# Queries times states in three bfloat16 parts on 32 columns per sequence, and state updates on 32 rows per sequence, in one layer of an mLSTM and convolution decoder

## The chip, the cores and the metric

The kernel runs on one core of a Trainium2 chip. The metric is the device time of one execution in microseconds, the median of several runs. Where a time inside the execution is given, it is counted from the start of the profiled span.

## The reference

One layer projects 512 prompt tokens and 64 sample tokens (8 sequences of 8 new tokens) with one matrix, runs an mLSTM over 4 heads of 256 on one half of the columns and a gated causal convolution on the other half, and projects the result. The change touches the mLSTM of the sample tokens. Each of their 8 sequences brings a state per head, a 256 x 256 matrix C and a vector n. With q, k, v of the 8 new tokens the reference computes

```
s   = (q @ k.T) * exp(dmat - m_t)
num = w_inter * (q @ C) + s @ v
den = w_inter * (q @ n) + sum(s)
h   = num / max(|den|, exp(-m_t))
C_new = decay * C + sum_s ws[s] * outer(k[s], v[s])
n_new = decay * n + sum_s ws[s] * k[s]
```

followed by a layer norm over each head. The new states are outputs. All inputs and outputs are float32.

## The kernel before

TensorE works on float32 data with float32r matmuls: every operand is split into a high part and the rest, and a product is the sum of three matmuls (high x high, high x rest, rest x high). The split is an `activation` copy on ScalarE into the high part and a subtraction on VectorE for the rest.

The program is written as one list in the order of the main projection. `ORDER` names 61 column tiles; for each tile (a "unit of 16") the loop in lines 892 to 904 runs k from 0 to 15. One k is six matmuls (`proj`, line 184): three of 256 columns and three of 320. At every fourth k, ahead of the matmuls, `split` (lines 76 to 90) splits the weights that are due 12 k later: ScalarE L85, VectorE L86, with rings of `RING = 4` buffers; every second split also issues a weight load on SP (`load`). After k = 15, `evac` copies or gates the tile out of PSUM on ScalarE (L200, L202, L757) and VectorE (L763).

Everything else is hung into this list by `at(s, k, f)`: function f is issued behind the matmuls of tile s, index k (lines 656 to 700). No scheduler moves anything: each engine executes its instructions in the order in which they are issued, and waits where an operand or a buffer is not ready. In what follows, step n of a head is the n-th k counted from the one at which `b_SV(h, 0)` stands, `o` in line 687 (for heads 1 to 3 a weight split falls on steps 2, 6, 10 and so on and an `evac` between steps 5 and 6 and between 21 and 22; for head 0 splits fall on steps 0, 4, 8 and evacs ahead of steps 8 and 24).

For one head, the steps that matter here are: `b_SV` (prompt scores times values, L549) at steps 0 to 6, `head_ln` (layer norm of the prompt rows, line 572) at step 7, `b_KV` (L557) at 8 and 10, `b_hT` (transposes, L598) at 14 and 16. For the sample tokens `b_q` (line 455) writes the scaled queries into `QM`, high part in columns 0 to 7 and rest in columns 64 to 71 of a 128-column block per sequence. `c_split` (line 377) splits a state into `Chi` and `Clo`. `b_sC` (line 603), once per sequence b at steps 12, 16, ... 40, multiplies shifted windows of `QM` with both parts (L611, four matmuls of 258 columns, all 128 rows and columns), so that all sequences accumulate in one PSUM tile `ns`; the first call adds the in-chunk part (`Es` times `vs`, L614). Every second call also makes the state updates of two sequences (L623: four matmuls of 32 rows x 128 columns, 256 columns of right side), VectorE merges them with the decayed states (L629), POOL stores them (L630) and SP loads the next two states. `b_sLN` (line 634) copies `ns` out at step 42, moves its lower 64 rows to the upper ones with a DMA, and does the layer norm at step 48; `b_shT` follows at step 66. Small PSUM tiles `mi` rotate through three buffers.

Of the kernel before, what the change touches and what calls it, by code (L numbers as in the profile page):

```python
# [6 lines left out]

F32 = mybir.dt.float32
F32R = mybir.dt.float32r
AF = mybir.ActivationFunctionType  # L10
OP = mybir.AluOpType
PSUM = bass.MemoryType.PSUM

P = 128
# [3 lines left out]
NB, T8 = 8, 8  # L18
TS = NB * T8
# [3 lines left out]
NH = 4  # L23
DH = 256
# [31 lines left out]
def hybrid(ctx, tc, x0, wg0, wu, wgate, cpack, gpack, sct, hist, xres, lnp,  # L56
           o_y, o_ys, o_C, o_m, o_cs, o_ns, o_ms, o_cv, o_cvs):
    nc = tc.nc
    pe, act, dve, pool = nc.tensor, nc.scalar, nc.vector, nc.gpsimd
    main = ctx.enter_context(tc.tile_pool(name="main", bufs=1))  # L60
    dramp = ctx.enter_context(tc.tile_pool(name="dram", bufs=1, space=bass.MemoryType.DRAM))
# [91 lines left out]
    def mi(shape=(P, 512)):  # L153
        return psum.tile(list(shape), F32, name="mi", tag="mi", bufs=3)
# [7 lines left out]
    def ns_tile():  # L162
        return psum.tile([P, 512], F32, name="ns", tag="ns", bufs=1)
# [24 lines left out]
    KQV = {}  # L188
# [16 lines left out]
    g0t = new_phase("g0")  # L205
# [6 lines left out]
            nc.sync.dma_start(xr[k], x0[k])  # L212
            nc.sync.dma_start(wr[k], wg0[k])

    warm = g0t([P, 512], mybir.dt.bfloat16, "warm")
    dve.memset(warm, 1.0)
    wps = ns_tile()
    for _ in range(8):
# [47 lines left out]
    for k in range(KT):  # L266
        for n, x in enumerate((XH, XL)):
            for b in range(2):
                c0, c1 = SPANS[b]
# [97 lines left out]


    m = {}
    CS, CH = {}, {}  # L370

    def c_load(i):
        if i < NH * NB:
            CS[i] = m["t"]([P, 2, 258], F32, "Ct", bufs=5)
            nc.sync.dma_start(CS[i], sct[i])

    def c_split(i):
        if i < NH * NB:
            CH[i] = [m["t"]([P, 2, 258], F32R, n, bufs=2) for n in ("Chi", "Clo")]
            act.activation(CH[i][0], CS[i], AF.Copy)  # L380
            dve.tensor_sub(CH[i][1], CS[i], CH[i][0])  # L381

    def rb_load(h):
        m["RB"] = m["t"]([P, TOK + TS], F32, "RB")
# [5 lines left out]
    def open_m():  # L390
        t = m["t"] = new_phase("m2")
        m["vs"] = t([TS, 258], F32, "vs")
        m["QM"] = t([P, 2 * NB, P], F32R, "QM")
        pool.memset(m["vs"][:, 256:257], 1.0)
        pool.memset(m["vs"][:, 257:258], 0.0)
        pool.memset(m["QM"].bitcast(F32), 0.0)
        rb_load(0)
        for i in range(5):
            c_load(i)

    def b_E(h, part):
# [52 lines left out]

    def b_q(h):

        q, QM = KQV["q", h], m["QM"]
        qw = m["t"]([P, 2, TS], F32, "qw")
        for d in range(2):
            pool.tensor_tensor(out=qw[:, d], in0=q[:, d, S:], in1=m["RB"][:, TOK:], op=OP.mult)  # L460
        qv = qw.rearrange("p d (b t) -> p (d b) t", t=T8)
        act.activation(QM[:, :, 0:T8], qv, AF.Copy)
        dve.tensor_sub(QM[:, :, TS:TS + T8], qv, QM[:, :, 0:T8])

    def b_kT(h, a):
        if a == 0:
# [133 lines left out]
        hT[e] = mt([P, TOK], F32, f"hT{e}", tag="hT", bufs=8)  # L600
        act.activation(hT[e][:, :S], ps, AF.Copy, scale=hn_g[:, e:e + 1])

    def b_sC(h, b):
        if b == 0:
            m["ns"] = ns_tile()
        i = NB * h + b
        ch, cl = CH.pop(i)
        for d in range(2):
            w = m["QM"].rearrange("p a c -> p (a c)")[:, d * NB * P + b * 120:d * NB * P + b * 120 + P]
            for n, c in enumerate((ch, cl)):  # L610
                pe.matmul(m["ns"][:, :258], lhsT=w, rhs=c[:, d], start=b == 0 and d == 0 and n == 0,  # L611
                          stop=b == NB - 1 and d == 1 and n == 1)
            if b == 0 and d == 0:
                pe.matmul(m["ns"][:TS, :258], lhsT=m["Es"], rhs=m["vs"], start=False, stop=False)  # L614
        c_split(i + 1)
        if b % 2 == 0:
            return
        pss = []
        for bb in (b - 1, b):
            g, j = divmod(bb, 4)  # L620
            ps = mi((P, 2, DH))
            for d in range(2):
                pe.matmul(ps[:, d], lhsT=m["kS"][32 * j:32 * j + 32, g, d * P:(d + 1) * P],  # L623
                          rhs=m["vS"][32 * j:32 * j + 32, g], start=True, stop=True)
            pss.append(ps)
        for bb, ps in zip((b - 1, b), pss):
            ct = CS.pop(NB * h + bb)
            c = ct[:, :, :DH]
            dve.scalar_tensor_tensor(c, c, m["dec", h][:, bb:bb + 1], ps, op0=OP.mult, op1=OP.add)  # L629
            pool.dma_start(o_cs[NB * h + bb], c)  # L630
        c_load(i + 4)
        c_load(i + 5)

    def b_sLN(h, part):
        if part == 0:
            nsb, m["t2"] = m["t"]([P, 1, 258], F32, "nsb"), m["t"]([TS, 258], F32, "nsl")
            act.activation(nsb[:, 0], m["ns"][:, :258], AF.Copy)
            act.dma_start(m["t2"], nsb[TS:, 0])
            m["nsb"] = nsb
        else:  # L640
            nums = m["nums"] = m["nsb"][:TS]
            dve.tensor_add(nums[:, 0], nums[:, 0], m["t2"])
            head_ln(nums, TS, 1, CTs[:, 1, h:h + 1])

    def b_shT(h):
# [10 lines left out]
    def at(s, k, f, *a):  # L656
        s, k = s + k // KT, k % KT
        beside.setdefault((s, k), []).append((f, a))
# [5 lines left out]
    for h in range(NH):  # L664
# [27 lines left out]
        at(o[0], o[1] + 10, b_KV, h, 1)  # L692
        at(o[0], o[1] + 14, b_hT, h, 0)
        at(o[0], o[1] + 16, b_hT, h, 1)
        at(o[0], o[1] + 5, c_split, NB * h)
        for i in range(NB):
            at(o[0], o[1] + 12 + 4 * i, b_sC, h, i)
        at(o[0], o[1] + 42, b_sLN, h, 0)
        at(o[0], o[1] + 48, b_sLN, h, 1)
        at(o[0], o[1] + 66, b_shT, h)  # L700


# [402 lines left out]
```

## Time and profile before

| | before |
|---|---|
| median of 3 runs | 1145.35 us (1145.32 to 1145.37) |
| profiled execution | 1145.27 us |
| its span | 1143.3 us, 19722 instructions |
| TensorE busy | 1130.3 us, 99% of the span |
| VectorE busy | 722.0 us, 63% |
| ScalarE busy | 406.1 us, 36% |
| GpSimd busy | 147.0 us, 13% |

The span is the time from the first to the last instruction that the profiler recorded. Busy times count overlapping instructions once. Matmuls are pipelined, so the duration of one (some 0.3 us) is longer than the distance to the next.

### The profile page before, as it was taken

How to read it: one execution, taken by the hardware profiler on the slowest of the kernel's cores; microseconds unless marked ns; L12 is line 12 of the kernel's file. 1: busy time of each engine (PE TensorE's matmuls, PEld its weight loads, DVE VectorE, ACT ScalarE, POOL GpSimd, SP SyncE). 2: the span in 40 equal slices, each digit the busy share in tenths (PEclk: the TensorE clock that was granted, in tenths of full speed). 3: DMA queues.
4: the chain of work that ended last, by engine and by line, in shares of the span. 5: the costliest groups of instructions: out<-in, count | busy, mean ns of one | idle time of the engine just before them, and what ended most of it. 6: DMA issues, size and time to landing. Idle time of an engine off the chain costs nothing.

```text
span 1143.3 us, 19722 instructions
## 1 busy us (share of the span) xinstructions
PE 1130.3 (99%) x8062; PEld 1085.9 (95%) x8062; DVE 722.0 (63%) x1207; ACT 406.1 (36%) x772; POOL 147.0 (13%) x217
## 2 busy tenths in 40 slices
PE   9999999999999999999999999999999999999996
PEld 8999999999999999999999999999999988888895
DVE  6385455455355445428899998999977872433447
ACT  5335453345344443422222222222236651221224
POOL 0022030011002003101010111111203310000004
PEclk9999999999999999999999999999999999999998
DMA  8114262253245224222223222222222246632229
GB/s 292 68 57 132 77 195 86 77 185 96 74 134 168 67 74 160 86 87 90 93 92 108 87 100 85 85 81 75 93 93 75 92 145 188 205 143 93 70 87 166
DMA packets 43659, 127.50 MB, mean 112 GB/s; under 512 B 5372, under 2 KB 10108, under 8 KB 43120
## 3 DMA queue, kind: packets, MB, share of 16 engines
q1 hardware_dynamic: 37712, 112.44, 30.0%
q0 software_dynamic: 4992, 12.94, 4.3%
q8 instruction: 63, 1.03, 0.4%
q10 hardware_dynamic: 864, 0.85, 0.3%
q14 instruction: 28, 0.23, 0.1%
HBM read 110.11 MB, written 18.72 MB: 113 GB/s over the span
## 4 chain that ended last, share of the span: by engine, by line
PE 99%; DVE 1%; issue 0%; DVEq 0%
PE pp L184 71%; PE pp L977 3%; PE pp L978 3%; PE pp L979 3%; PE mi L978 2%; PE mi L979 2%; PE mi L977 2%; PE ns L611 1%; PE mi L442 1%; PE mi L974 1%; PE mi L973 1%; PE mi L549 1%; PE mi L184 1%; PE mi L557 1%; PE mi L623 1%; PE ns L979 0%
## 5 line engine op out<-in xcount | busy, mean ns | idle before, releaser
L184 PE MATMUL pp<-xh,whi 128*128 128x256 f32 (+1 forms) x1952 | 423.3, 298 | 0.0
L184 PE MATMUL pp<-xl,whi 128*128 128x256 f32 (+1 forms) x1952 | 416.5, 295 | 0.0
L184 PE MATMUL pp<-xh,wlo 128*128 128x256 f32 (+1 forms) x1952 | 415.5, 295 | 0.0
L86 DVE TENSOR_TENSOR wlo<-raw,whi 128x512 fp32r<-128x512 f32 x300 | 221.8, 742 | 266.9 <-ACT whi L85 266.5
L85 ACT ACTIVATE whi<-raw 128x512 fp32r<-128x512 f32 x300 | 188.5, 632 | 391.9 <-PE pp L184 246.1
L184 PEld LDWEIGHTS pp<-xh,wlo 128*128 128x128 f32 x1952 | 326.7, 188 | 0.0
L184 PEld LDWEIGHTS pp<-xl,whi 128*128 128x128 f32 x1952 | 326.4, 188 | 0.0
L184 PEld LDWEIGHTS pp<-xh,whi 128*128 128x128 f32 x1952 | 321.6, 189 | 3.0 <-issue 0.3
L724 DVE SCALAR_TENSOR_TENSOR Y<-U,cp,Y 128x512 f32<-128x512 f32 x240 | 189.8, 791 | 5.3
L978 PE MATMUL pp<-whi,mx 128*128 128x512 f32 (+1 forms) x128 | 46.9, 366 | 0.0
L977 PE MATMUL pp<-whi,mx 128*128 128x512 f32 (+1 forms) x128 | 46.9, 366 | 0.0
L979 PE MATMUL pp<-wlo,mx 128*128 128x512 f32 (+1 forms) x128 | 46.8, 366 | 0.0
L630 POOL DMA_DIRECT2D o_cs<-Ct x32 | 22.5, 717 | 181.9 <-DVE Ct L629 181.9
L381 DVE TENSOR_TENSOR Clo<-Ct,Chi 128x516 fp32r<-128x516 f32 x35 | 25.7, 733 | 27.4 <-ACT Chi L380 27.4
L757 ACT ACTIVATE sg<-pp,cp 128x256 f32<-128x256 f32 (+1 forms) x48 | 21.4, 496 | 45.4 <-PE pp L184 45.4
L978 PE MATMUL mi<-whi,mx 128*128 128x512 f32 (+1 forms) x96 | 36.1, 376 | 0.0
L977 PE MATMUL mi<-whi,mx 128*128 128x512 f32 (+1 forms) x96 | 36.0, 375 | 0.0
L979 PE MATMUL mi<-wlo,mx 128*128 128x512 f32 (+1 forms) x96 | 36.0, 375 | 0.0
L979 PEld LDWEIGHTS pp<-wlo,mx 128*128 128x128 f32 x128 | 24.1, 188 | 4.3
L977 PEld LDWEIGHTS pp<-whi,mx 128*128 128x128 f32 x128 | 24.1, 188 | 4.3
L978 PEld LDWEIGHTS pp<-whi,mx 128*128 128x128 f32 x128 | 24.0, 188 | 4.3
L1005 POOL DMA_DIRECT2D o_ys<-zs x4 | 3.4, 1184 | 188.9 <-ACT zs L1004 188.9
(334 smaller groups left out, 1370.1 us busy)
## 6 DMA issues: line engine op xcount, KB each, us to landing
raw<-wu SPq DMA_DIRECT2D x154, 512.0 KB, 3.3
Ct<-sct SPq DMA_DIRECT2D x32, 258.0 KB, 2.8
o_cs<-Ct POOLq DMA_DIRECT2D x32, 256.0 KB, 2.8
xr<-x SPq DMA_DIRECT2D x16, 288.0 KB, 5.0
z<-xres SPq DMA_DIRECT2D x8, 512.0 KB, 5.9
wr<-wg SPq DMA_DIRECT2D x16, 192.0 KB, 5.1
o_y<-z POOLq DMA_DIRECT2D x11, 256.0 KB, 7.6
o_y<-lnp SPq DMA_DIRECT2D x2, 1024.0 KB, 10.0
```

The costliest lines, as they stand in the source:

```text
L85: act.activation(hi, r, AF.Copy)
L86: (eng or dve).tensor_tensor(out=lo, in0=r, in1=hi, op=OP.subtract)
L184: pe.matmul(out[b], lhsT=w, rhs=x[:, slice(*SPANS[b])], start=k == 0 and n < 2, stop=k == KT - 1 and n >= 4)
L381: dve.tensor_sub(CH[i][1], CS[i], CH[i][0])
L442: pe.matmul(dst[J], lhsT=m[k_][:, d, J * P:(J + 1) * P], rhs=m[q_][:, d, J * P:S], start=d == 0 and n == 0, stop=d == 1 and n == 2)
L549: pe.matmul(ps[:, :258], lhsT=m[p_][:, o:o + P], rhs=m[v_][:, J], start=J == 0 and n == 0, stop=J == I and n == 2)
L630: pool.dma_start(o_cs[NB * h + bb], c)
L724: dve.scalar_tensor_tensor(y, u, w, y, op0=OP.mult, op1=OP.add)
L757: act.activation(sg[:, c0:c1], ps, AF.Sigmoid, bias=b_in[:, c:c + 1])
L977: pe.matmul(ps, lhsT=h_, rhs=hi, start=first, stop=False)
L978: pe.matmul(ps, lhsT=l_, rhs=hi, start=False, stop=False)
L979: pe.matmul(ps, lhsT=h_, rhs=lo, start=False, stop=last)
```

## The change

The queries are split into three bfloat16 parts (`Q`: 24 of 32 columns per sequence and d), and so is each state (`c0`, `c1`, `c2`, made by `c_split` with two ScalarE and two VectorE operations). `b_qC(h, r)` handles four sequences at once: each sequence's 32 query columns are the stationary operand on its own strip of 32 columns of TensorE's array, and its three parts stream by; rows 0 to 7, 8 to 15 and 16 to 23 of a strip collect the products of the three query parts. The result goes to SBUF, by DMA to `nsd` in DRAM, and comes back as three [64, 258] terms (`n3`), which are added to `nums`. `b_sKV(h, r)` makes the state updates of four sequences, in an order in which neighbouring matmuls lie on different 32-row strips and in different PSUM banks. `c_load` has eight buffers instead of five; `c_next` loads four states of the next head.

```diff
-    CS, CH = {}, {}
+    CS = {}
+    nsd = [dramp.tile([4, 4, T8, 2, 258], F32, name=f"nsd{h}") for h in range(NH)]
...
-            CS[i] = m["t"]([P, 2, 258], F32, "Ct", bufs=5)
+            CS[i] = m["t"]([P, 2, 258], F32, "Ct", bufs=8)
...
     def c_split(i):
-        if i < NH * NB:
-            CH[i] = [m["t"]([P, 2, 258], F32R, n, bufs=2) for n in ("Chi", "Clo")]
-            act.activation(CH[i][0], CS[i], AF.Copy)
-            dve.tensor_sub(CH[i][1], CS[i], CH[i][0])
+        j = i % 4
+        if j == 0:
+            for n, tag in (("c0", "Ph"), ("c1", "Pl"), ("c2", None)):
+                m[n] = m["t"]([P, 4, 2, 258], BF16, n, tag=tag)
+        c0, c1, c2 = (m[n][:, j] for n in ("c0", "c1", "c2"))
+        r = m["t"]([P, 2, 258], F32, "cr")
+        act.activation(c0, CS[i], AF.Copy)
+        dve.tensor_sub(r, CS[i], c0)
+        act.activation(c1, r, AF.Copy)
+        dve.tensor_sub(c2, r, c1)
...
     def b_q(h):
-        act.activation(QM[:, :, 0:T8], qv, AF.Copy)
-        dve.tensor_sub(QM[:, :, TS:TS + T8], qv, QM[:, :, 0:T8])
+        p_ = [Q.rearrange("p d b c -> p (d b) c")[:, :, i * T8:(i + 1) * T8] for i in range(3)]
+        act.activation(p_[0], qv, AF.Copy)
+        dve.tensor_sub(qv, qv, p_[0])
+        act.activation(p_[1], qv, AF.Copy)
+        dve.tensor_sub(p_[2], qv, p_[1])
...
-    def b_sC(h, b):
...
+    def b_qC(h, r):
+        if r == 0:
+            m["nsb"] = m["t"]([P, 2, 258], F32, "nsb")
+        ps = mi()
         for d in range(2):
+            for n in ("c0", "c1", "c2"):
+                for j in range(4):
+                    pe.matmul(ps[32 * j:32 * j + 32, :258], lhsT=m["Q"][:, d, 4 * r + j], rhs=m[n][:, j, d],
+                              start=d == 0 and n == "c0", stop=d == 1 and n == "c2")
+        act.activation(m["nsb"][:, r], ps[:, :258], AF.Copy)
+        if r:
+            act.dma_start(nsd[h].rearrange("j i t r e -> (j i t) r e"), m["nsb"])
+
+    def b_sKV(h, r):
+        pss = [mi((P, 2, DH)) for _ in range(3)] + [ns_tile().rearrange("p (d e) -> p d e", d=2)]
+        for d in range(2):
+            for j in range(4):
+                rows = slice(32 * j, 32 * j + 32)
+                pe.matmul(pss[j][:, d], lhsT=m["kS"][rows, r, d * P:(d + 1) * P], rhs=m["vS"][rows, r],
+                          start=True, stop=True)
+        for j in range(4):
+            b = 4 * r + j
+            c = CS.pop(NB * h + b)[:, :, :DH]
+            dve.scalar_tensor_tensor(c, c, m["dec", h][:, b:b + 1], pss[j], op0=OP.mult, op1=OP.add)
+            pool.dma_start(o_cs[NB * h + b], c)
+
+    def c_next(h, r):
+        for j in range(4):
+            c_load(NB * (h + 1) + 4 * r + j)
...
     def b_sLN(h, part):
         if part == 0:
-            nsb, m["t2"] = m["t"]([P, 1, 258], F32, "nsb"), m["t"]([TS, 258], F32, "nsl")
-            act.activation(nsb[:, 0], m["ns"][:, :258], AF.Copy)
-            act.dma_start(m["t2"], nsb[TS:, 0])
+            ps = mi()
+            pe.matmul(ps[:TS, :258], lhsT=m["Es"], rhs=m["vs"], start=True, stop=True)
+            m["nums"] = m["t"]([TS, 1, 258], F32, "nums")
+            act.activation(m["nums"][:, 0], ps[:TS, :258], AF.Copy)
+        elif part == 1:
+            m["n3"] = m["t"]([TS, 3, 258], F32, "n3", tag="cr")
+            for r in range(2):
+                for j in range(4):
+                    b = 4 * r + j
+                    nc.sync.dma_start(m["n3"][b * T8:(b + 1) * T8], nsd[h][j, :3, :, r].rearrange("i t e -> t i e"))
...
-        at(o[0], o[1] + 5, c_split, NB * h)
-        for i in range(NB):
-            at(o[0], o[1] + 12 + 4 * i, b_sC, h, i)
-        at(o[0], o[1] + 42, b_sLN, h, 0)
-        at(o[0], o[1] + 48, b_sLN, h, 1)
+        for r in range(2):
+            for j in range(4):
+                at(o[0], o[1] + (7, 19)[r] + (0, 1, 2, 4)[j], c_split, NB * h + 4 * r + j)
+            at(o[0], o[1] + (18, 31)[r], b_qC, h, r)
+            at(o[0], o[1] + (21, 35)[r], b_sKV, h, r)
+            at(o[0], o[1] + (27, 41)[r], c_next, h, r)
+        at(o[0], o[1] + 25, b_sLN, h, 0)
+        at(o[0], o[1] + 42, b_sLN, h, 1)
+        at(o[0], o[1] + 52, b_sLN, h, 2)
```

ScalarE's order in head 1 from the layer norm of the prompt rows (`sm`) on, before the change (`kv` and `hT` are evictions, `whi` a weight split, `q` a projection tile's eviction):

```order
L566 ACTIVATE sm_2699<-sm_2699 128x4
L560 ACTIVATE kv<-mi 128x258
L85 ACTIVATE whi<-raw 128x512
L560 ACTIVATE kv<-mi 128x258
L380 ACTIVATE Chi<-Ct 128x516
L85 ACTIVATE whi<-raw 128x512
L601 ACTIVATE hT_2826<-mi,cp 128x512
L601 ACTIVATE hT_2845<-mi,cp 128x512
L380 ACTIVATE Chi<-Ct 128x516
L85 ACTIVATE whi<-raw 128x512
```

The same place in the changed kernel (`c_2778` is `c0`, `c_2779` is `c1` of the first four states):

```order
L578 ACTIVATE sm_2750<-sm_2750 128x4
L387 ACTIVATE c_2778<-Ct 128x516
L389 ACTIVATE c_2779<-cr 128x516
L572 ACTIVATE kv<-mi 128x258
L387 ACTIVATE c_2778<-Ct 128x516
L389 ACTIVATE c_2779<-cr 128x516
L387 ACTIVATE c_2778<-Ct 128x516
L389 ACTIVATE c_2779<-cr 128x516
L86 ACTIVATE whi<-raw 128x512
L572 ACTIVATE kv<-mi 128x258
L387 ACTIVATE c_2778<-Ct 128x516
L389 ACTIVATE c_2779<-cr 128x516
```

Four splits of states, two operations each, now stand together behind the layer norm, ahead of the evictions and weight splits that stood there.

VectorE's order in head 1 from the last operation of the layer norm on, before the change (`wlo` is a weight split):

```order
L592 TENSOR_SCALAR num<-num,mv_2701,sm_2699 128x256 x4
L86 TENSOR_TENSOR wlo<-raw,whi 128x512
L381 TENSOR_TENSOR Clo<-Ct,Chi 128x516
L86 TENSOR_TENSOR wlo<-raw,whi 128x512
L381 TENSOR_TENSOR Clo<-Ct,Chi 128x516
L629 SCALAR_TENSOR_TENSOR Ct<-Ct,dec,mi 128x2x256 x2
```

The second four states in the changed kernel (`cr` is `r`, `c_2962` is `c2`):

```order
L87 TENSOR_TENSOR wlo<-raw,whi 128x512 x2
L388 TENSOR_TENSOR cr<-Ct,c_2960 128x516
L390 TENSOR_TENSOR c_2962<-cr,c_2961 128x516
L388 TENSOR_TENSOR cr<-Ct,c_2960 128x516
L390 TENSOR_TENSOR c_2962<-cr,c_2961 128x516
L640 SCALAR_TENSOR_TENSOR Ct<-Ct,dec,mi 128x2x256 x3
L640 SCALAR_TENSOR_TENSOR Ct<-Ct,dec,ns 128x2x256
L388 TENSOR_TENSOR cr<-Ct,c_2960 128x516
L390 TENSOR_TENSOR c_2962<-cr,c_2961 128x516
L87 TENSOR_TENSOR wlo<-raw,whi 128x512
L388 TENSOR_TENSOR cr<-Ct,c_2960 128x516
L390 TENSOR_TENSOR c_2962<-cr,c_2961 128x516
```

The state updates of the first four sequences stand in the middle of the splits of the second four.

## Rows read from the trace of the kernel before

**Rows 1.** Page: span, busy time of each engine, engines of the chain that ended last.
```profile
span 1143.3 us, 19722 instructions
...
PE 1130.3 (99%) x8062; PEld 1085.9 (95%) x8062; DVE 722.0 (63%) x1207; ACT 406.1 (36%) x772; POOL 147.0 (13%) x217
...
PE 99%; DVE 1%; issue 0%; DVEq 0%
```

**Rows 2.** TensorE's groups by shape: instructions x count, busy us, mean ns, idle before.
```profile
L611 PE MATMUL ns<-Chi,QM 128*128 128x258 f32 x64 | 17.6, 295 | 0.0
L611 PE MATMUL ns<-Clo,QM 128*128 128x258 f32 x64 | 16.9, 282 | 0.0
...
L623 PE MATMUL mi<-vS,kS 32*128 32x256 f32 x64 | 8.1, 328 | 0.0
```

**Rows 3.** Timeline of TensorE, head 1, steps 12 to 17: start us, length us, what.
```profile
224.69 0.28 PE L611 MATMUL ns<-Chi,QM 128*128 128x258 f32 x1
...
225.94 0.43 PE L184 MATMUL pp<-xh,whi 128*128 128x256 f32 x2
...
227.54 0.60 PE L598 MATMUL mi<-ident,num 128*128 128x128 f32 x4
227.89 0.51 PE L184 MATMUL pp<-xh,whi 128*128 128x256 f32 x2
...
230.24 0.28 PE L611 MATMUL ns<-Chi,QM 128*128 128x258 f32 x1
230.35 0.28 PE L611 MATMUL ns<-Clo,QM 128*128 128x258 f32 x1
230.56 0.50 PE L623 MATMUL mi<-vS,kS 32*128 32x256 f32 x4
231.00 0.53 PE L184 MATMUL pp<-xh,whi 128*128 128x256 f32 x2
231.37 0.42 PE L184 MATMUL pp<-xl,whi 128*128 128x256 f32 x2
```

**Rows 4.** Timeline of VectorE, head 1, last operation of the layer norm on.
```profile
221.29 1.38 DVE L592 TENSOR_SCALAR num<-num,mv,sm 128x256 f32<-128x256 f32 x4
222.59 0.69 DVE L86 TENSOR_TENSOR wlo<-raw,whi 128x512 fp32r<-128x512 f32 x1
224.28 0.69 DVE L381 TENSOR_TENSOR Clo<-Ct,Chi 128x516 fp32r<-128x516 f32 x1 [1.00 <-ACT Chi L380]
...
232.06 1.40 DVE L629 SCALAR_TENSOR_TENSOR Ct<-Ct,dec,mi 128x512 f32<-128x512 f32 x2
```

**Rows 5.** Timeline of ScalarE, head 1.
```profile
223.62 0.63 ACT L380 ACTIVATE Chi<-Ct 128x516 fp32r<-128x516 f32 x1
...
235.74 0.89 ACT L202 ACTIVATE q<-pp,cp 128x256 f32<-128x256 f32 x2 [2.75 <-PE pp L184]
```

**Rows 6.** Timelines, heads 0 and 3: end of the layer norm, step 13, table load.
```profile
133.14 1.39 DVE L592 TENSOR_SCALAR num<-num,mv,sm 128x256 f32<-128x256 f32 x4
...
136.92 0.28 PE L611 MATMUL ns<-Chi,QM 128*128 128x258 f32 x1
...
422.39 0.28 PE L611 MATMUL ns<-Chi,QM 128*128 128x258 f32 x1
...
422.51 1.38 DVE L592 TENSOR_SCALAR num<-num,mv,sm 128x256 f32<-128x256 f32 x4
...
430.71 1.28 ACT L757 ACT_TABLE_LOAD   x1
```

**Rows 7.** Page, DMA issues: KB each, median us from issue to landing.
```profile
raw<-wu SPq DMA_DIRECT2D x154, 512.0 KB, 3.3
```

**Rows 8.** Stretches: us, busy us of each engine (instructions), granted clock, DMA.
```profile
205.00:255.00 50.00, 50.00 (x383) 48.37 (x382) 24.81 (x55) 19.90 (x40) 4.20 (x6) 1.00 0.41 128
...
1134.00:1136.00 2.00, 0.00 (x0) 0.00 (x0) 1.93 (x7) 0.00 (x0) 0.00 (x0) 1.00 1.10 221
1136.00:1138.00 2.00, 0.00 (x0) 0.00 (x0) 2.00 (x3) 0.00 (x0) 0.00 (x0) 0.60 1.09 237
```

More of the change, by code (lines that the diff above doesn't have):

```diff
@@ L9 @@
 F32R = mybir.dt.float32r
+BF16 = mybir.dt.bfloat16
 AF = mybir.ActivationFunctionType
@@ L213, in g0_load @@
             nc.sync.dma_start(wr[k], wg0[k])
-    warm = g0t([P, 512], mybir.dt.bfloat16, "warm")
+    warm = g0t([P, 512], BF16, "warm")
     dve.memset(warm, 1.0)
@@ L392, in open_m @@
         m["vs"] = t([TS, 258], F32, "vs")
-        m["QM"] = t([P, 2 * NB, P], F32R, "QM")
+        m["Q"] = t([P, 2, NB, 32], BF16, "Q")
         pool.memset(m["vs"][:, 256:257], 1.0)
         pool.memset(m["vs"][:, 257:258], 0.0)
-        pool.memset(m["QM"].bitcast(F32), 0.0)
+        pool.memset(m["Q"], 0.0)
         rb_load(0)
-        for i in range(5):
+        for i in range(8):
             c_load(i)
@@ L455, in b_q @@
     def b_q(h):
-        q, QM = KQV["q", h], m["QM"]
+        q, Q = KQV["q", h], m["Q"]
         qw = m["t"]([P, 2, TS], F32, "qw")
@@ L601, in b_hT @@
         act.activation(hT[e][:, :S], ps, AF.Copy, scale=hn_g[:, e:e + 1])
-    def b_sC(h, b):
[L604 to L607, printed above, removed]
-        for d in range(2):
[L609 to L632, printed above, removed]
@@ L634, in b_sLN @@
+    def c_next(h, r):
+        for j in range(4):
+            c_load(NB * (h + 1) + 4 * r + j)
     def b_sLN(h, part):
         if part == 0:
-            nsb, m["t2"] = m["t"]([P, 1, 258], F32, "nsb"), m["t"]([TS, 258], F32, "nsl")
-            act.activation(nsb[:, 0], m["ns"][:, :258], AF.Copy)
-            act.dma_start(m["t2"], nsb[TS:, 0])
-            m["nsb"] = nsb
-        else:
-            nums = m["nums"] = m["nsb"][:TS]
-            dve.tensor_add(nums[:, 0], nums[:, 0], m["t2"])
+            ps = mi()
[8 more added lines that the diff above has]
+                    nc.sync.dma_start(m["n3"][b * T8:(b + 1) * T8], nsd[h][j, :3, :, r].rearrange("i t e -> t i e"))
+        else:
+            nums = m["nums"]
+            for i in range(3):
+                dve.tensor_add(nums[:, 0], nums[:, 0], m["n3"][:, i])
```

## The prediction

> **What bounds the kernel.** I read the page first: TensorE is busy for 99% of the span, and the chain that ended last is 99% PE [rows 1]. So the time changes only by what TensorE executes or waits for, and any new wait costs its full length. I then read TensorE's groups by shape. The work that the change replaces is 128 queries-times-states matmuls (L611) and 64 state updates (L623) [rows 2]. Their durations, 282 to 328 ns, overlap and are no price; the price is the distance between starts, from the timeline of head 1 [rows 3]. Times inside a head are counted in steps: step n is the n-th k-step of the projection after `b_SV(h, 0)`, six matmuls long. Two steps take 227.54 - 225.94 = 1.60 us, so one takes 0.80. Consecutive L611 start 0.11 to 0.12 us apart (230.24, 230.35): 0.12.
>
> An L623 block has four matmuls, two on each of two row strips. All four fit into 0.50 us from first start to last end. At 0.12 us spacing plus the last one's 0.28 they would need 0.64, so matmuls on different row strips do run side by side here: four take about two rounds. The block delays the stream by more than its rounds. After L611 at 230.35 the pair `xl,whi` would start at 230.35 + 0.12 + 0.265 (a third of a step) = 230.74; it starts at 231.37. A block costs 0.63, of which 2 x 0.12 are rounds and 0.39 is going into and out of the small tiles [rows 3].
>
> Last, the DVE and ScalarE timelines of the same head. They show how long a split of a state takes: 0.63 on ScalarE, 0.03 later 0.69 to 0.70 on VectorE [rows 4, 5], and where the next op of an engine starts, some 0.1 before the last one ends. Each split feeds its matmuls steps later, so nothing waits for it now.
>
> **TensorE's own work.** Removed: 128 L611 at 0.12 = 15.4 us, and 16 L623 blocks at 0.63 = 10.1; together 25.5. Added: 8 `b_sKV` blocks. Each has eight matmuls, two on each of four row strips with a PSUM bank per strip; taken as two rounds like the block of today, 0.64, together 5.1. The other bound, strips two by two, is 0.63 + 2 x 0.12 = 0.87, together 7.0. Added: 8 `b_qC` blocks of 24 matmuls (two d, three parts, four sequences), each with a 258-column right side. No row shows matmuls on column strips side by side. If they run four at a time as the row strips do two at a time, a block is six rounds: 0.39 + 6 x 0.12 = 1.11, together 8.9. If not, 0.39 + 24 x 0.12 = 3.27, together 26.2. I take the first, since the L623 row is the nearest and shows that strips overlap. The `Es` matmul moves from the first L611 group to step 25. Today it takes 225.94 - 224.69 = 1.25 less four L611 = 0.77, tile changes included [rows 3]; it also needs them in its new place: 0. TensorE's work shrinks by 25.5 - 5.1 - 8.9 = 11.5 us, 2.9 per head.
>
> The Trainium skill, TensorE: Matmul & The Clock Gate, Part 3, reports less than full overlap: three column tiles gave 2.38 times. By that, as an estimate, the 24 matmuls of a block would take 1.21 instead of 0.72. No run here shows it.
>
> **The new chain.** The gain has to be set against `c_split`. Today a state needs one ScalarE and one VectorE op. Now it needs c0 (ScalarE), r (VectorE), c1 (ScalarE), c2 (VectorE), each reading the one before, with a single buffer for r, so the next r also waits for c2. The order rows show them back to back on both engines, and behind head_ln. I price all four as today's two (0.63 and 0.70, same 516 elements; the nearest rows). A state then takes r 0.70 + 0.03 + c1 0.63 + 0.03 + c2 0.70 + 0.03 = 2.12 us, and c0 of the next state hides under c2. A group of four takes 8.5 us, and no engine's idle time shortens it.
>
> *Head 1, first group.* The last L592 of head_ln lets VectorE go at 222.59 [rows 4]; the first r starts there. Between the states ScalarE's order has a kv eviction (0.05 late) and, before the fourth c0, a weight split and the other kv eviction; the fourth r is 0.6 late. The last c2 ends at 222.6 + 8.5 + 0.65 = 231.8. Only the c2 matmul of the fourth sequence and the twelve of d = 1 are still to come: 0.03 + 4 rounds x 0.12 + 0.1 out of the tiles, and projection goes on at 232.4. TensorE would get there earlier: step 13 starts at 224.69 once the first L611 group is gone, six steps and two transposing blocks of 0.35 (227.54 to 227.89) give 230.2, plus 1.1 for the block, 231.3. It waits 1.1.
>
> *Head 1, second group.* c0, c1, c2 are the same buffers, so it starts after the first block. ScalarE has two weight splits, two hT evictions and the block's own eviction in front (c0 done at 234.1). Two states end at 238.4; then VectorE's order has the four state updates, 0.66 apart (1.40 a pair [rows 4]), to 241.0; the third state ends at 243.0. Before the fourth c0 ScalarE has the projection's eviction (0.89) and a weight split [rows 5], so the last c2 ends at 246.3 and projection goes on at 246.9. TensorE alone would be there at 232.4 + 13 x 0.80 + 0.64 + 0.77 + 1.11 = 245.3. It waits 1.6, a part of that before `Es`, whose PSUM buffer is freed by the first state update.
>
> Head 1 thus waits 2.7 and gains 2.9. Head 2 is taken as equal. In head 0 the chain may start at 134.45 (133.14 + 1.39, less the 0.08 by which ops overlap) and TensorE's step 13 at 136.92 [rows 6], 0.35 more slack than head 1; but a projection eviction and a weight split lie between its first and second state (1.35), and only the kv eviction before the fourth. Waits 1.5 and 2.1, together 3.6. In head 3 head_ln ends late: L592 starts 0.12 after step 13's start (422.51 against 422.39) where head 1 has it 3.4 before, because sigmoids force table loads around head_ln. The split of a state at step 5, ahead of it on ScalarE, is gone in the change (0.5, one ScalarE op), so its first group is 3.0 later than head 1's: wait 4.1. Its second group has a table load of 1.28 [rows 6] and two gate ops in front of the last state: 3.4. Together 7.5. All heads: 3.6 + 2.7 + 2.7 + 7.5 = 16.5.
>
> **Edits at nothing.** VectorE gets 32 and ScalarE 32 more ops of this kind; beyond the chain they delay weight splits, which are issued 12 steps (9.6 us) before use and so cover some 3 us. SP gets the state loads in fours behind the landing of the stored states, and 32 small reads of `nsd`; weight loads behind them come up to 3 us late. A weight load lands in 3.3 us [rows 7] and its split is due 12 steps later, so about 3 us are still free; without that cover each us of lateness is a us of TensorE. `b_sLN` has ten steps between its read and its use. Memory for `CH` and `QM` goes, nothing waits on it.
>
> **Sum.** 16.5 - 11.5 = +5.0 us. The profiled execution took 1145.27 (span 1143.3 and 2.0 around it), 0.08 under the median of the runs: forecast **1150.3 us**. About 0.2% (2.3 us) is what a measurement of this kernel can tell from no change.
>
> **Rivals.**
> *The parts come in time: faster.* If the ops that read or write bfloat16 took 0.40 instead of 0.70, a state would take 1.5 and head 1's first group 6.7, ready at 229.3, before TensorE needs it at 230.2. The point from which this decides is a state under 1.75 us. Waits would remain in head 3 (about 2.0) and in second groups (about 0.5 each): 1145.3 - 11.5 + 3.5 = 1137. For it: half the bytes. Against: every op of two tensors in these rows takes 0.69 to 0.70 for 512 or 516 elements. The Trainium skill, VectorE: DVE Perf Modes, Mode 2×_1P, has the doubled rate of a two-tensor op only where operands are 16-bit; here Ct and r are 32-bit, so by it this rival falls too. Chance 0.18.
>
> *Column strips don't overlap: much slower.* What lies behind the last c2 is then 13 matmuls, 1.56 instead of 0.48, in eight blocks: +8.7, 1159. Half an overlap gives 1154. Chance 0.13.
>
> *TensorE's clock falls in a wait.* It was at its full level, 2.4 GHz, around head 1. At the end of the program a stretch without a matmul (1134 to 1136) still has it; in the next it falls towards the low level, 1.2 GHz (mean 0.60) [rows 8]. Head 3's first wait is 4.1 us, broken by the c0 and c1 matmuls, so I think it holds. If not, four steps at half speed cost 3.2: 1153.5. The Trainium skill, TensorE: Matmul & The Clock Gate, Part 1, has the clock gated down after idling, which is this case. Chance 0.12.
>
> **How the numbers follow.** The forecast, with waits of 12 to 20 us in all, has the remaining chance 0.57. Its uncertainty is eight chains of 0.5 us each way, 1146 to 1155; in its low corner the result is no change. Same: 0.12, faster: 0.20 (the first rival and a little of the corner), slower: 0.68. The range reaches from 1140, between the rival on the fast side and the forecast, to 1159.
>
> **What would show it.** The page after should have PE idle before the `b_qC` line, some 15 us in total, ended by DVE c2; starts of four `b_qC` matmuls nearly together, six rounds per block; a state's four ops 2.1 us from r to r; head 3's idle time the longest. It is wrong if PE stays at 99% (first rival), if `b_qC` matmuls start 0.11 apart (second), or if the granted clock drops after a wait (third).

## The result and the profile after

The changed kernel took **1155.26 us** (median of four runs, 1152.29 to 1156.85), the kernel before 1145.34 beside it: a ratio of 1.0085, interval 1.0062 to 1.0108. It is slower by 9.9 us, where +5.0 was forecast; the profiled pair, 1154.01 against 1145.27, differs by 8.7. The runs of the changed kernel lie further apart than those of before (4.6 us against 0.6).

The page after, in the same parts as [rows 1], with the granted clock by slices of 28.8 us:
```profile
span 1152.3 us, 19959 instructions
...
PE 1125.2 (98%) x8126; PEld 1073.8 (93%) x8126; DVE 749.1 (65%) x1248; ACT 424.2 (37%) x813; POOL 147.5 (13%) x217
...
PEclk9999999999999998999999999999999999999998
...
PE 77%; issue 11%; DVE 5%; ACT 3%; DMA 2%; POOL 1%; DVEq 0%; POOLq 0%; ACTq 0%
```
TensorE is busy for 5.1 us less, and the span is 9.0 us longer: it now waits. The chain was PE for 99% and now passes through VectorE, ScalarE, DMAs and GpSimd. Besides the last slice, which has it before the change too, one slice, in head 3, has a lower clock.

The new groups of TensorE and two of the split's operations (count, busy us, mean ns, idle before and what ended it), in place of [rows 2]:
```profile
L623 PE MATMUL mi<-c,Q 128*32 128x258 bf16 x192 | 11.0, 289 | 10.4 <-ACT c L389 4.9 <-DVE c L390 3.5 <-ACT kv L572 1.7
L650 PE MATMUL mi<-vs,Es 64*64 64x258 f32 x8 | 2.6, 403 | 2.2 <-DVE Ct L640 2.2
L389 ACT ACTIVATE c<-cr 128x516 bf16<-128x516 f32 x32 | 20.3, 634 | 46.9 <-DVE cr L388 46.9
L390 DVE TENSOR_TENSOR c<-cr,c 128x516 bf16<-128x516 f32 x32 | 22.7, 711 | 22.4 <-ACT c L389 21.0 <-PE ns L635 1.4
```
`b_qC` (L623) has 10.4 us of idle time before it, `Es` 2.2. c1 (L389) and c2 (L390) have the durations that were taken for them.

TensorE in head 1, first group (answers to [rows 3]):
```profile
231.32 0.40 PE L623 MATMUL mi<-c,Q 128*32 128x258 bf16 x7
232.00 0.29 PE L623 MATMUL mi<-c,Q 128*32 128x258 bf16 x4 [0.28 <-ACT c L389]
232.73 0.60 PE L623 MATMUL mi<-c,Q 128*32 128x258 bf16 x13 [0.44 <-DVE c L390]
233.26 0.53 PE L185 MATMUL pp<-xh,whi 128*128 128x256 f32 x2
...
235.84 0.39 PE L635 MATMUL mi<-vS,kS 32*128 32x256 f32 x3
235.85 0.38 PE L635 MATMUL ns<-vS,kS 32*128 32x256 f32 x1
```
The block comes in pieces, as its parts come: seven matmuls, four after the last c1, thirteen after the last c2. The thirteen take 0.53 us to the next projection, so four strips go together; so do the four row strips of `b_sKV`, 0.01 apart. VectorE's chain behind it (answers to [rows 4]):
```profile
223.49 0.69 DVE L388 TENSOR_TENSOR cr<-Ct,c 128x516 f32<-128x516 f32 x1
224.88 0.70 DVE L390 TENSOR_TENSOR c<-cr,c 128x516 bf16<-128x516 f32 x1 [0.70 <-ACT c L389]
225.68 0.69 DVE L388 TENSOR_TENSOR cr<-Ct,c 128x516 f32<-128x516 f32 x1
...
231.98 0.70 DVE L390 TENSOR_TENSOR c<-cr,c 128x516 bf16<-128x516 f32 x1 [0.70 <-ACT c L389]
```
From r to r 2.19 us (2.12 forecast). The last c2 ends at 232.68, and TensorE goes on at 232.73.

**Where the time went.** The start of the same projection matmul in both traces (the 769th, for example) gives what each stretch gained or lost: head 0 +1.1 us; head 1 -0.1; then +1.3 while the keys of head 2 are prepared; head 2 -0.2; +1.4 at the keys of head 3; head 3 +5.9. The sum is +9.4; 0.3 was gained ahead of head 0, and 0.1 comes back after the last projection, which makes the 9.0 by which the spans differ.

*The two stretches between heads.* The timelines of SP, VectorE, ScalarE and TensorE, between heads 1 and 2:
```profile
256.23 3.10 SPq L377 DMA_DIRECT2D Ct<-sct  x4
259.38 5.24 SPq L658 DMA_DIRECT2D n<-nsd  x8
```
```profile
266.10 1.33 DVE L662 TENSOR_TENSOR nums<-nums,n 64x258 f32<-64x258 f32 x3 [1.48 <-DMA n<-nsd]
```
```profile
269.09 0.20 ACT L577 ACTIVATE sm<-sm 64x1 f32<-64x1 f32 x1 [5.20 <-DVE sm L600]
...
269.44 0.87 ACT L201 ACTIVATE k<-pp,bk 128x256 f32<-128x256 f32 x2
...
270.73 1.14 ACT L438 ACTIVATE kh<-k 128x512 fp32r<-128x512 f32 x2
```
```profile
271.40 0.50 PE L451 MATMUL mi<-qh,kh 128*128 128x512 f32 x1 [0.50 <-ACT kh L438]
```
SP's four state loads stand ahead of the eight reads of `nsd`; the reads land late, VectorE waits 1.48 for them, the samples' layer norm begins at 266.10, and ScalarE waits 5.20 us for its middle at 269.09. Behind that stand the eviction of k and its split kh, and TensorE waits for kh at the queries times keys (L451, QK in what follows).

*Head 3, first group* (answers to [rows 6, 8]): TensorE, one row of ScalarE, and stretches with the granted clock.
```profile
431.07 0.42 PE L185 MATMUL pp<-xh,wlo 128*128 128x256 f32 x2
433.21 0.29 PE L623 MATMUL mi<-c,Q 128*32 128x258 bf16 x3 [1.71 <-ACT kv L572]
433.73 0.29 PE L623 MATMUL mi<-c,Q 128*32 128x258 bf16 x4 [0.23 <-ACT c L387]
435.12 0.41 PE L623 MATMUL mi<-c,Q 128*32 128x258 bf16 x4 [1.10 <-ACT c L389]
435.86 1.02 PE L623 MATMUL mi<-c,Q 128*32 128x258 bf16 x13 [0.33 <-DVE c L390]
436.81 0.85 PE L185 MATMUL pp<-xh,whi 128*128 128x256 f32 x2
...
437.94 0.68 PE L185 MATMUL pp<-xh,wlo 128*128 128x256 f32 x2
438.42 0.68 PE L185 MATMUL pp<-xh,whi 128*128 128x256 f32 x2
```
```profile
432.79 0.37 ACT L572 ACTIVATE kv<-mi 128x258 f32<-128x258 f32 x1
```
```profile
429.00:435.00 6.00, 3.08 (x27) 2.56 (x26) 3.89 (x6) 3.66 (x8) 0.00 (x0) 1.00 0.13 44
...
437.00:438.00 1.00, 1.00 (x5) 1.00 (x6) 0.69 (x1) 1.00 (x3) 0.00 (x0) 0.50 0.24 74
```
The first 1.71 is a wait for a PSUM tile: the kv eviction that frees it stands on ScalarE behind three states' splits. Then c0, c1 and c2 of the fourth state are waited for. The granted clock falls to 0.50, its lower level, and a pair of projection matmuls takes 0.48 us from start to start (437.94, 438.42) instead of 0.27.

*Head 3, second group.* The subtraction that makes the fourth state's r takes 1.92 us and not 0.69, and a GpSimd operation runs beside it:
```profile
449.99 1.92 DVE L388 TENSOR_TENSOR cr<-Ct,c 128x516 f32<-128x516 f32 x1
```
```profile
449.62 1.73 POOL L802 TENSOR_TENSOR hT<-hT,sg 128x576 f32<-128x576 f32 x1 [3.45 <-DVE sg L787]
```
In all twelve traces, that of the kernel before included, a subtraction of a state's split beside which GpSimd computes nothing takes at most 0.70 us, and every longer one runs while GpSimd computes. That GpSimd is the reason was not tested.

### The profile page after: what moved, and what is told of

Read it like the earlier page. It is cut to its first block, busy times and chain, and to the rows that moved or that the text cites. A ratio compares the mean times of both kernels' runs of the same rounds, so it can differ in the third digit from the quotient of the medians.

```text
span 1152.3 us, 19959 instructions
## 1 busy us (share of the span) xinstructions
PE 1125.2 (98%) x8126; PEld 1073.8 (93%) x8126; DVE 749.1 (65%) x1248; ACT 424.2 (37%) x813; POOL 147.5 (13%) x217
## 4 chain that ended last, share of the span: by engine, by line
PE 77%; issue 11%; DVE 5%; ACT 3%; DMA 2%; POOL 1%; DVEq 0%; POOLq 0%; ACTq 0%
PE pp L185 54%; PE pp L1001 3%; PE pp L1003 3%; PE pp L1002 3%; PE mi L1002 2%; PE mi L1003 2%; PE mi L1001 2%; PE mi L997 1%; PE mi L998 1%; PE mi L451 1%; PE mi L185 1%; DVE cr L388 1%; DMA Ct<-sct 1%; POOL o_cs L641 1%; DMA o_cs<-Ct 1%
## 5 line engine op out<-in xcount | busy, mean ns | idle before, releaser
L389 ACT ACTIVATE c<-cr 128x516 bf16<-128x516 f32 x32 | 20.3, 634 | 46.9 <-DVE cr L388 46.9
L390 DVE TENSOR_TENSOR c<-cr,c 128x516 bf16<-128x516 f32 x32 | 22.7, 711 | 22.4 <-ACT c L389 21.0
```

The source lines that it names most:

```text
L389: act.activation(c1, r, AF.Copy)
L390: dve.tensor_sub(c2, r, c1)
```

## The experiments

The theory after the result: TensorE's own work shrank as priced; what is lost is (a) waits for the chain of splits, (b) the late layer norm of the samples, (c) the clock in head 3. The rivals are that the new blocks cost more than priced, and that the waits come from elsewhere. Times are medians; each interval is of 95%, and each ratio is to the kernel before on the same chip.

### 1. The samples' layer norm later

```diff
-        at(o[0], o[1] + 52, b_sLN, h, 2)
-        at(o[0], o[1] + 66, b_shT, h)
+        at(o[0], o[1] + 70, b_sLN, h, 2)
+        at(o[0], o[1] + 79, b_shT, h)
```


> Edit: of the change, only the second part of the samples' layer norm moves from step 52 to 70 of a head and the transposes of its result from 66 to 79. Theory (in the changed kernel's trace the QK matmuls of heads 2 and 3 wait because VectorE and ScalarE do that layer norm just ahead of the splits of k; the two idle times are 0.50 + 0.28 and 0.57 + 0.28 us, and the run falls back by 1.3 and 1.4 us there): both stalls go, 2.7 us less than the changed kernel, about 1152.5. Rival (the splits of k are late because of the weight loads that SP issues behind the stored states): the stalls stay, about 1155.

1155.66 us, ratio 1.0088 (1.0073 to 1.0103): no gain. But the waits at L451 are gone, and new ones stand at the transposes of the result (`b_shT`), in heads 1, 2 and 3:
```profile
293.33 0.30 PE L668 MATMUL mi<-ident,nums 64*128 64x64 f32 x2 [0.86 <-DVE nums L604]
```
The wait at QK hangs on the layer norm's place, as the theory has it, and nine steps behind it are too few for its result. The gain was spent there, and this execution lost 1.5 us more in head 3 than that of the changed kernel (experiment 5 has the reason).

### 2. The loads of the next head's states later

```diff
-            at(o[0], o[1] + (27, 41)[r], c_next, h, r)
+            at(o[0], o[1] + (44, 56)[r], c_next, h, r)
```


> Edit: of the change, only the loads of the next head's states move, from steps 27 and 41 to 44 and 56, behind the reads of the samples' parts at 42; one buffer for r, all else as in the change. Theory (the reads of the samples' parts were late because they stand on SP's queue behind state loads that wait for stored states to land, 256.2 to 259.4 in head 1): the reads land by 258, the layer norm starts about 1.5 us earlier, when VectorE's order comes to it, and the two waits at QK of heads 2 and 3 shrink from 1.3 and 1.4 to under 0.4: 1153 to 1154 against 1155.3, and in the trace the first DVE add of the parts has no idle time ended by a DMA. Rival (the layer norm is late by its place in VectorE's order): the two waits stay.

1153.75 us, ratio 1.0069 (1.0052 to 1.0086). SP and VectorE between heads 1 and 2:
```profile
256.87 4.54 SPq L658 DMA_DIRECT2D n<-nsd  x8
```
```profile
265.13 1.32 DVE L662 TENSOR_TENSOR nums<-nums,n 64x258 f32<-64x258 f32 x3
```
Ahead of the loads the reads land in time: L662 waits for no DMA, and from this and the stretch between heads 2 and 3 the loss of 1.3 and 1.4 us is gone (0.0 and 0.0 by the same projection matmuls). The median gained 1.5 and not 2.7; in this profile head 3 lost 8.5 us instead of 5.9, with the clock down in both of its groups (experiment 5 has what that costs). That SP's order made the layer norm late is shown, with 2.7 us by the projection matmuls; the medians can't confirm the price, in runs this far apart (1151.6 to 1154.61).

### 3. Two buffers for r

```diff
-        c0, c1, c2 = (m[n][:, j] for n in ("c0", "c1", "c2"))
-        r = m["t"]([P, 2, 258], F32, "cr")
-        act.activation(c0, CS[i], AF.Copy)
-        dve.tensor_sub(r, CS[i], c0)
-        act.activation(c1, r, AF.Copy)
-        dve.tensor_sub(c2, r, c1)
+        r = m["t"]([P, 2, 258], F32, "cr", bufs=2)
+        act.activation(m["c0"][:, j], CS[i], AF.Copy)
+        dve.tensor_sub(r, CS[i], m["c0"][:, j])
+        if j:
+            c_rest()
+        m["cj"] = r, j
+        if j == 3:
+            c_rest()
```
`c_rest` holds the two removed operations, for the r kept in `m["cj"]`: c1 and c2 come one state later. The tile of the samples' parts moves to the buffer of c2, so that both r fit.

> Edit: two buffers for r, and c1 and c2 of a state are issued after c0 and r of the next state; steps and blocks stay where the change puts them. Theory (the waits are the chain of four ops that each read the one before, 2.2 us from r to r): VectorE then does r and c2 back to back, 1.40 to 1.45 us a state, a group of four is ready 2 us earlier, waits of up to 2 us ahead of the blocks of heads 0 to 2 vanish (2.5 + 2.9 + 2.9 us), head 3 loses 4 to 7 us of its own with the clock's fall; the two stalls at QK (2.7) stay: 1140 to 1146. Rival (what is waited for is the engines' other work ahead of the splits, in order, and not the chain): less than 4 us, 1151 to 1155.

**1134.28 us**, ratio 0.9904 (0.9888 to 0.9921): faster than both kernels, by more than expected. VectorE and TensorE in head 1:
```profile
219.11 1.30 DVE L387 TENSOR_TENSOR cr<-Ct,c 128x516 f32<-128x516 f32 x2
220.50 0.70 DVE L397 TENSOR_TENSOR c<-cr,c 128x516 bf16<-128x516 f32 x1
221.30 0.70 DVE L387 TENSOR_TENSOR cr<-Ct,c 128x516 f32<-128x516 f32 x1
```
```profile
226.93 0.84 PE L630 MATMUL mi<-c,Q 128*32 128x258 bf16 x24
```
No VectorE operation waits for c1 any more, the steps are those of the change, and the block runs in one piece. Of the 10.4 us of idle time before `b_qC` 0.7 is left. That the chain of four dependent operations is what TensorE waited for is shown. Some 1.5 us of the gain lie elsewhere (last section).

### 4. The same chain, later blocks

```diff
+        q0 = 28 if h == 3 else 23
...
-            at(o[0], o[1] + (18, 31)[r], b_qC, h, r)
...
+            at(o[0], o[1] + q0 + 20 * r, b_qC, h, r)
```
and what stands behind it, as the text on record says.

> Edit: splits as in the change, but the blocks stand later: queries times states at steps 23 and 43 (head 3: 28 and 48) instead of 18 and 31, the second group's splits behind the first block, state updates 3 and 4 steps behind their block, the layer norm of samples and its transposes at 70 and 79, loads of the next head's states at 36 and 62. Same operations, same chain. Theory (TensorE's own work shrank by 11.5 us, all of which and more went into waits that only the steps make): no wait is left, 1145.3 - 11.5 = 1133.8, within 1132 to 1137, and faster than the kernel before. Rival (the new blocks cost TensorE more than priced, that is a block of queries times states over 1.1 or of states over 0.64): 1138 to 1144. Second rival (stalls move to the next head's QK or to head 3's end): over 1140 with PE idle there.

1139.64 us, ratio 0.9953 (0.9938 to 0.9968): faster than before, but 2.6 us short of the theory's range. By the number alone the first rival would hold; the trace is against it, since each block of queries times states delays the projection by 0.98 us, less than the 1.1 that was priced. No idle time is left before `b_qC`. Three others took its place: `Es` 3.1 us in all (its PSUM tiles are freed by state updates that stand behind the second group's splits on VectorE), `b_shT` 3.0 (as in experiment 1), and 1.1 at QK of head 1, which state updates end too. The second rival holds in part: the waits of the change went, and the steps chosen made new ones.

### 5. Matmuls of no use in head 3's waits

```diff
+                fill(h, r, d, n)
                 for j in range(4):
```
`fill` issues matmuls of `kwh` and `vh` into a PSUM tile of its own, ahead of head 3's first block, at d = 0.

> Edit: in head 3's first block of queries times states, 16, 9 and 5 extra matmuls of 256 columns into a PSUM tile that nobody reads, ahead of its first rounds of c0, c1 and c2, where TensorE waits 1.9, 1.4 and 0.7 us in the changed kernel. They add work of no use, 30 x 0.11 = 3.3 us, nearly all inside waits. Theory (the granted clock falls to its lower level because of these waits, and four steps at 1.44 instead of 0.80 us and six rounds at 0.2 instead of 0.1 us are then 3 us of loss): the clock stays at 1.00 from 435 to 441 and the time is 2 to 3 us less, 1152 to 1153, and spreads less from run to run. Rival (the clock falls for another reason, or its fall costs nothing since the chain is what is waited for): the same time as the changed kernel or up to 0.8 us more, 1155 to 1156.

1158.76 us, ratio 1.0119 (1.0104 to 1.0134): worse than the changed kernel, outside both ranges. The extra matmuls took a tile of the same three PSUM tiles and waited as long as the block would have (2.02 us from start to start), so the block ended 2.5 us later, counted from the 2401st projection matmul, and the second group's splits, which reuse its buffers, 2.2 us later. The clock stayed at 1.00 from 430 to 442, and fell in the second group instead (0.57 from 454 to 458). With the bank of `ns`, which is free by then, and in both groups:

> Edit: the changed kernel with 23 and 33 extra matmuls of 256 columns in head 3's two blocks of queries times states (12, 8, 3 and 14, 16, 3 ahead of the first rounds of c0, c1, c2), into a PSUM bank that is free by then, so that they don't wait for an eviction; nobody reads them. They are 56 x 0.11 = 6.2 us of work of no use, inside the waits as far as these reach. Theory now (the fall of the clock in head 3 makes TensorE later, but the second group's splits end when they end, so what the fall costs is taken off the second wait): the granted clock stays at 1.00 in head 3, and the time is that of the changed kernel within 1.5 us, 1154 to 1156. Rival (the fall adds its 3 us to the time, as the prediction priced it): 1151 to 1153.

1155.38 us, ratio 1.0089 (1.0074 to 1.0104). The stretch that was at 0.50 in the changed kernel, and the first projection after the second group (first this run, then the changed kernel):
```profile
438.00:442.00 4.00, 4.00 (x43) 3.54 (x33) 2.23 (x4) 2.96 (x6) 0.00 (x0) 1.00 0.36 131
```
```profile
455.66 0.53 PE L185 MATMUL pp<-xh,whi 128*128 128x256 f32 x2
```
```profile
453.88 0.53 PE L185 MATMUL pp<-xh,whi 128*128 128x256 f32 x2
```
This execution was 1.73 us behind before head 3 (the 2401st projection matmul starts at 417.54 against 415.81), and it is 1.78 behind here. With and without the fall, head 3's second group ends at the same time, since its splits end when they end. So (c) falls for the changed kernel's profiled execution: the clock's fall was real and cost nothing there.

A fall behind the second group does cost. In the changed kernel, experiment 1 and experiment 2 the last c2 of head 3 ends 37.5 us behind the 2401st projection matmul; but in the last two the clock is down behind it, no other wait follows, and the 2737th projection matmul comes 64.1 and 65.3 us behind the 2401st instead of 62.6, that is 1.5 and 2.7 later. TensorE in experiment 2, then in the changed kernel (stretch, busy us, granted clock, DMA):
```profile
454.00:458.00 4.00, 4.00 (x23) 0.59 0.52 183
```
```profile
454.00:458.00 4.00, 4.00 (x34) 1.00 0.57 199
```

### 6. All waits taken out, first try, and the state updates alone

```diff
-            at(o[0], o[1] + (27, 41)[r], c_next, h, r)
...
-        at(o[0], o[1] + 42, b_sLN, h, 1)
-        at(o[0], o[1] + 52, b_sLN, h, 2)
+            at(o[0], o[1] + (44, 56)[r], c_next, h, r)
...
+        at(o[0], o[1] + (42 if h == 3 else 38), b_sLN, h, 1)
+        at(o[0], o[1] + (52 if h == 3 else 46), b_sLN, h, 2)
```
on top of experiment 3, and head 3's blocks two steps later.

> Edit: two buffers for r and c1, c2 of a state behind c0, r of the next (as in the run with two buffers); in heads 0 to 2 the reads of the samples' parts move from step 42 to 38 and their layer norm from 52 to 46, ahead of the splits of k and of the loads of the next head's states, which move to 44 and 56; head 3's blocks move two steps back, 20 and 33. Theory (what idle time is left with two buffers is the wait at QK of heads 2 and 3, 0.82 + 0.69 and 0.68 + 0.68 us from start to start, behind the late layer norm, and 0.50 + 0.72 in head 3): these go, 3.4 us less than 1134.3: about 1131. Rival (the layer norm at 46 only shifts the wait to another line): 1133 to 1135.

1136.9 us, ratio 0.9929 (0.9915 to 0.9944): 2.6 worse than experiment 3, against the theory and outside the rival's range too. ScalarE between heads 1 and 2, and `Es` in head 3:
```profile
257.92 0.20 ACT L584 ACTIVATE sm<-sm 64x1 f32<-64x1 f32 x1 [5.29 <-DVE sm L607]
...
261.96 0.87 ACT L201 ACTIVATE k<-pp,bk 128x256 f32<-128x256 f32 x2
```
```profile
431.57 0.65 PE L657 MATMUL mi<-vs,Es 64*64 64x258 f32 x2 [3.23 <-DVE Ct L647]
```
The layer norm at step 46 has ScalarE wait 5.29 us, and now the exponentials of the next head stand behind it, and k's eviction behind them: QK waits as before. In head 3 the state updates, two steps later, come behind the gating of a projection tile on VectorE, which waits 1.51 us for ScalarE, and free the tiles for `Es` late.

The same kernel with the old state updates, two blocks of two strips for a group:
```diff
-        pss = [mi((P, 2, DH)) for _ in range(3)] + [ns_tile().rearrange("p (d e) -> p d e", d=2)]
+        pss = [mi((P, 2, DH)) for _ in range(2)]
```


> Edit: as the run before it in this list, but the state updates stand as before the change: sixteen blocks of four matmuls on two row strips, two PSUM banks each, the second of a group two steps behind the first. Theory (a block costs 0.63 us whether two or four strips run in it; with four strips there are half as many): 16 x 0.63 - 8 x 0.64 = 5.0 us more than with four strips, about 1136. Rival (four strips take two by two, 0.87 a block): 10.1 - 7.0 = 3.1 more, 1134. Second rival (the blocks' price lies in their matmuls and not in going into and out of the small tiles): 0 to 1 more.

1141.57 us, 4.7 more (ratio to the kernel before 0.9969, 0.9957 to 0.9981). Inside heads 0, 1 and 2, ahead of the waits at QK, the same projection matmuls fall back by 1.24, 1.25 and 1.25 us a head: 5.0 for four heads. A block delays the projection by 0.67 to 0.68 us from start to start around it, with two strips as with four: four strips cost what two did, and the first theory holds. That the median comes near 5.0 is luck in part: 1.7 us are made up again at the waits at QK, and head 3 loses 2.0, with a wait of 2.83 us ahead of a state update that the four-strip kernel doesn't have.

### 7. The combined kernel, and its blocks strip by strip

```diff
-        at(o[0], o[1] + 25, b_sLN, h, 0)
...
-        at(o[0], o[1] + 52, b_sLN, h, 2)
-        at(o[0], o[1] + 66, b_shT, h)
+        at(o[0], o[1] + (17 if h == 3 else 25), b_sLN, h, 0)
...
+        at(o[0], o[1] + (52 if h == 3 else 70), b_sLN, h, 2)
+        at(o[0], o[1] + (66 if h == 3 else 88), b_shT, h)
```
on top of experiment 3, with head 3's blocks at 20 and 33.

> Edit: two buffers for r and c1, c2 of a state behind c0, r of the next; in heads 0 to 2 the samples' layer norm moves behind the next head's splits of k and its transposes (step 70) and the transposes of its result to 88, clear of it by 18 steps; in head 3 the first block moves from step 18 to 20, its second from 31 to 33, with their state updates, and the Es matmul from 25 to 17, ahead of the state updates whose PSUM tiles it waited for. The rest as in the change. Theory (with two buffers 1134.3 was left with waits of 1.3 and 1.1 at QK of heads 2 and 3, by the layer norm's place on ScalarE and VectorE, and of 1.0 in head 3's first block): no idle time of TensorE over 0.3 us in heads 0 to 3, 1130.5 to 1132. Rival (the waits move again to another line): 1133 to 1137.

**1132.18 us**, ratio 0.9887 (0.9872 to 0.9902), 13 us under the kernel before and 23 under the changed one, with the same work. Its page:
```profile
PE 1115.9 (99%) x8126; PEld 1069.9 (95%) x8126; DVE 747.1 (66%) x1248; ACT 424.0 (38%) x813; POOL 147.1 (13%) x217
...
PE 98%; DVE 1%; ACT 0%; issue 0%; DVEq 0%
```
The chain is PE again. The waits at QK and `Es` are gone; 1.5 us of waits for c1 and c2 is left, in head 3's second group. A head without waits (0 to 2) gains 3.2 us.

The same kernel with `for j` outside `for d` and `for n` in `b_qC`:

> Edit: as the combined kernel, but a block of queries times states goes through its 24 matmuls strip by strip (all six of a sequence, then the next sequence) instead of part by part (four sequences side by side). Same matmuls, same results. Theory (it is the neighbours on different column strips that run at the same time, so that 24 matmuls take six rounds): strip by strip they take some 18 to 24 rounds of 0.11 us, 8 blocks x 12 to 18 x 0.11 = 11 to 16 us more than the combined kernel. Rival (matmuls on different strips overlap whatever their order): 0 to 3 us more.

1137.34 us, ratio 0.9933 (0.9916 to 0.9950), 5.2 more: between both. One block, side by side in the combined kernel and then strip by strip:
```profile
227.45 0.85 PE L630 MATMUL mi<-c,Q 128*32 128x258 bf16 x24
```
```profile
228.26 1.54 PE L630 MATMUL mi<-c,Q 128*32 128x258 bf16 x24
```
It takes 0.69 us more. In seven blocks that makes 4.9 us, about what was measured; the eighth, head 3's second, waits for c2 in either order. The order matters, and even strip by strip the strips overlap in part.

## Why the prediction was right, and where it was off

The sign and the reason hold: the work shrinks, and the waits for the splits take more than it gives. The size was half of what was measured, and 1155.26 lies at the edge of the 1146 to 1155 that the forecast gave its own uncertainty. By its own steps:

- **TensorE's own work, 11.5 us.** Right, a little low: 3.2 a head in the combined kernel, 12.7 in all, instead of 2.9. A `b_sKV` block delays projection by 0.64, as priced; a `b_qC` block by 0.98 instead of 1.11 (227.09 to 228.60 for two pairs of projection matmuls that take 0.53 without it, in the combined kernel).
- **The second rival, no overlap.** Out: six rounds of four, 0.10 to 0.11 apart, with 0.002 to 0.006 between strips. The Trainium skill, TensorE: Matmul & The Clock Gate, Part 3, has 2.38 for three tiles; here four gave nearly the full factor, and the measurement decides.
- **The first rival, parts in time.** Out: c1 took 0.63 and c2 0.71 although they write bfloat16. A state under 1.75 us did decide, as the rival had it, but it came by a second buffer (experiment 3).
- **The waits, 16.5 us.** Adding 3.2 of saved work to each stretch's loss gives 4.3 for head 0 (forecast 3.6), 3.1 and 3.0 for heads 1 and 2 (2.7 each), 9.1 for head 3 (7.5): 19.5. The mechanism and the order of the heads were right; the sizes were low. In head 3 the flat 0.70 for VectorE was one term too small: the subtraction of 1.92 us adds 1.2 to the second group's wait. A kv eviction behind the splits on ScalarE kept the first block's first matmul as well, but c2 of the fourth state, which ended at 435.81, set the block's end.
- **"`b_sLN` has ten steps between its read and its use."** This edit was costed at nothing, and it is the step that failed: 2.7 us. The steps were counted from where the read is issued in the program. On SP's queue it stood behind four loads that wait for stored states to land, which the prediction had named for weight loads alone.
- **The third rival, the clock.** "I think it holds" was wrong: the clock fell in the broken wait. Its price, +3.2, was not paid in the profiled execution: it came off the next wait. Falls behind the second group were paid, with 1.5 and 2.7 (experiment 5). The Trainium skill, TensorE: Matmul & The Clock Gate, Part 1, has the clock gated down after idling; the trace agrees, with 0.50 behind these waits.
- **The sum.** Waits of 19.5 and 2.7, less 12.7, are +9.5 where the forecast had 16.5 and 0, less 11.5. That the traces have +9.4 over these stretches is no second proof, since the waits were taken from them.

## What to carry to other kernels

When a matmul's operand becomes a chain of operations that hop between two engines with one buffer between them, price the chain and not the engines' busy time, and look first for a second buffer: here the same operations were 21 us faster with it, once c1 and c2 were issued one state later. A wait taken out by moving a step comes back where the moved work's result, its PSUM tile or its place in an engine's order is needed next; three of the moves here did that. A clock that falls in a wait costs nothing if the next wait is set by something else; where no such wait follows, it cost 1.5 to 2.7 us here.

## What was not expected

- **The clock does not fall each time.** In head 0 `Es` waits 1.71 us in the changed kernel and in experiment 5's second run; in the first the stretch 154 to 158 has 1.00, in the second 0.57:
```profile
154.00:158.00 4.00, 4.00 (x33) 4.00 (x32) 3.21 (x5) 1.16 (x2) 4.00 (x7) 1.00 0.76 262
```
```profile
154.00:158.00 4.00, 4.00 (x19) 4.00 (x20) 3.21 (x5) 1.16 (x2) 4.00 (x8) 0.57 0.70 242
```
  The fall cost 0.6 us of head 0 (+1.7 instead of +1.1 to the kernel before). How much of the 4.6 us between the runs of the changed kernel comes from such falls, and from those behind head 3's second group, stays open; the runs of experiment 4, in whose profile the clock stays up in heads 0 to 3, lie 0.45 apart.
- **Strip by strip is not one after the other.** 24 matmuls in that order took 1.27 us from first start to last instead of 0.57, and not 24 rounds of 0.11.
- **A shorter step.** In the five kernels with two buffers for r a step of the later projections (from the end of head 3 to about 835 us) takes 0.790 us; in all others, the kernel before too, 0.793. It is worth 1.5 us, and nothing tried here tells why.
